# Casts and low parts of the first-half output-projection weights kept behind earlier work of ScalarE and VectorE

## The chip, the cores and the metric

The kernel runs on one core of a Trainium2 chip. The metric is the device time of one execution in microseconds; the time of a kernel is the median of its runs.

## The reference

One inference step of a two-layer model with `D_MODEL` 1024: 128 context tokens and 512 latent tokens, 640 tokens (`T`) in all. In each layer four token mixers stand side by side (grouped-query attention, neighbourhood attention, gated DeltaNet, latent attention "MLA"); the head groups share one input projection and one output projection, and a SwiGLU channel mixer follows. The change touches the output projection alone:

```python
mixed = concat([o_gqa, o_na, o_dn, o_mla], -1)     # 1024 wide, in eight blocks of 128
x = x + gate * (mixed @ w_out)                     # 640 tokens x 1024
```

All matrices are 32-bit floats, and the products are computed to about that precision.

## The kernel before

Matrix products are made of three TensorE passes: each 32-bit operand is split into a rounded part and a low part (what is left), and high x high, high x low, low x high are added. A weight tile is therefore loaded by SyncE into `wst`, rounded by ScalarE into `whi` (line 309), and subtracted by VectorE into `wlo` (line 310). `weights` (line 312) issues these three. `wst` is a ring of three buffers in the pool `wp`; it also holds `xe`, below.

The mixed heads arrive in four pairs `oh` (0 to 3, two blocks of 128 each). The first four blocks are ready well before the last, so the output projection is cut in two. `half_out` (line 2118 on) does the first half while the attention of the latent tokens runs, one tile at a time: for tile `e` of 0 to 5 it loads `wout[l, e, :, 0:4]` (128x512), splits it, loads the residual stream `xe` into a buffer of the ring, makes two half steps of matmuls (256 tokens, then 384 tokens), adds the product to `xe` on VectorE (line 1937) and stores `xe` to scratch memory `dx` (line 2134). The loop over `order` behind the attention does the second halves (called second-half tiles here; six tiles of 128x512, then two whole ones of 128x1024), which read `dx` back into `x`.

TensorE's order is written out by a planner of the kernel: generators for each mixer and for `half_out` take turns by estimated times (`self.od`), and TensorE runs in exactly that order. The instructions of the other engines go to a scheduler, which may move an instruction ahead of others that its engine was given earlier, if its operands allow it. `in_turn` (line 304) marks an instruction that keeps its place in program order. In the kernel before, the split of every weight tile is free to move.

Around the tiles ScalarE runs the exponentials `p` (line 1421), the copies `pt` of transposed exponentials out of the accumulators (line 1456), norms and casts of the neighbourhood attention; VectorE runs row sums and maxima `sm`, reciprocals `sd`, mask additions, low parts and residuals; GpSimd scales (`dg`).

Of the kernel before, what the change touches and what calls it, by code (L numbers as in the profile page):

```python
# [11 lines left out]
F32 = mybir.dt.float32  # L12
# [3 lines left out]
ALU = mybir.AluOpType  # L16
# [272 lines left out]
class _Build:  # L289
# [19 lines left out]
        self.nc.scalar.copy(hi, src)  # L309
        self.nc.vector.tensor_tensor(out=lo, in0=src, in1=hi.bitcast(F32), op=ALU.subtract)  # L310

    def weights(self, src, shape, pool=None, bufs=2, parts=None):

        nc = self.nc
        st = self.wp.tile(shape, F32, tag="wst", name="wst", bufs=3)
        nc.sync.dma_start(out=st, in_=src)
        hi, lo = parts or [(pool or self.wp).tile(shape, F32R, tag=t, name=t, bufs=bufs) for t in ("whi", "wlo")]
        self.split(hi, lo, st)
        n = 1
        for d in shape[1:]:  # L320
            n *= d
        self.od.via(("ACT", 0.1 + n / 1200), ("DVE", 0.07 + n / 960))
        return hi, lo
# [1663 lines left out]
    def mixer(self, l, h, h_st, x, fx, fx_st, P, W, p_side, w_side):  # L1987


        nc, A = self.nc, self.A  # L1990
# [78 lines left out]
        def attention():  # L2069
# [36 lines left out]
            last.extend([od.spawn(self.mla(S, oh, at, ps, 3), 3), _Event()])  # L2106
            e = od.spawn(self.mla_operands(l, mp, mk, xp, ats, ps, S), 1.5)
            od.spawn(half_out(xp, ev_g), 7, True)
            yield e
            mp_st.close()  # L2110
# [5 lines left out]
        wout = lambda q, k: S["oh"][k // 2][:, q, k % 2]  # L2116

        def half_out(xp, ready):

            yield ready  # L2120
            for e in range(KD):
                if all(t.at is not None for t in last):
                    break
                halves.append(e)
                yield "wt", 1
                w = self.weights(A["wout"][l, e, :, 0:4], [128, 4, 128], xp)
                xe = self.wp.tile([128, T], F32, tag="wst", name="xe", bufs=3)
                nc.sync.dma_start(out=xe, in_=xs[:, e])
                for hf in range(2):
                    o = yield from self.half_steps(w, wout, range(4), hf, ps)  # L2130
                    self.residual(l, 2, e, {hf: o}, xe, xe)
                    od.give("fd", at=od.via(("DVE", 0.5)))
                od.give("wt")
                nc.sync.dma_start(out=self.dscr["x1"][:, e], in_=xe)
# [225 lines left out]
```

## Time and profile before

| what | value |
|---|---|
| time, median of 3 runs | 1942.76 us (1941.82 to 1942.79) |
| profiled execution | 1942.35 us, its span 1940.6 us |
| TensorE busy | 1820.8 us (94%) |
| VectorE busy | 1219.8 us (63%) |
| ScalarE busy | 784.7 us (40%) |
| GpSimd busy | 512.7 us (26%) |

The span is the time from the first to the last instruction of the profiled execution; the 1.75 us between it and that execution's time lie around it. Engines run side by side, so a busy time is no part of a sum. A row of a timeline ends with the idle time of its engine just before it and with the instruction that ended that time. The first layer's attention with the six tiles lies at about 320 to 510 us of the span, the second layer's at about 1255 to 1455 us.

### The profile page before, as it was taken

To read this page: it belongs to the slowest core of one execution; us is meant where nothing else is said; L and a number is where in the kernel's file an instruction comes from. 1 tells how busy PE (TensorE), PEld (TensorE's weight loads), DVE (VectorE), ACT (ScalarE), POOL (GpSimd) and SP (SyncE) were. 2 spreads that over 40 slices of the span, in tenths; PEclk is the share of its full clock that TensorE was granted. 3 is DMA by queue.
4 is the path that set the end of the run, shared out by engine and by line. 5 is a ranking of instruction groups with operands and counts; after the bars stand their busy time and mean duration, and the time that the engine had idled before them with its cause. 6 is when DMAs were issued, how large, how long until landed. Compare 5 with 4: busy or idle time off the path is not lost.

```text
span 1940.6 us, 40518 instructions
## 1 busy us (share of the span) xinstructions
PE 1820.8 (94%) x16392; PEld 1714.9 (88%) x16392; DVE 1219.8 (63%) x2488; ACT 784.7 (40%) x1627; POOL 512.7 (26%) x648
## 2 busy tenths in 40 slices
PE   5997998899999999999999999879989999999997
PEld 4986787778899999999998988768779999999997
DVE  6573546676557647747745773566757784774874
ACT  4632123676452212212337432267655541442541
POOL 1221431233220000000021363213324451642731
PEclk9997899999999999999999999989999999999999
DMA  8345323133435525625522232213432222222231
GB/s 302 113 123 135 120 91 98 36 95 88 150 109 176 161 84 181 184 77 192 173 100 92 73 92 66 73 37 78 106 129 89 66 88 76 88 80 82 78 97 55
DMA packets 114171, 210.38 MB, mean 108 GB/s; under 512 B 44160, under 2 KB 61312, under 8 KB 113856
## 3 DMA queue, kind: packets, MB, share of 16 engines
q1 hardware_dynamic: 105920, 202.74, 33.3%
q0 software_dynamic: 2816, 4.72, 1.2%
q8 instruction: 129, 2.11, 0.4%
q10 hardware_dynamic: 5248, 0.33, 0.2%
q14 instruction: 58, 0.48, 0.1%
HBM read 183.14 MB, written 19.89 MB: 105 GB/s over the span
## 4 chain that ended last, share of the span: by engine, by line
PE 77%; DVE 9%; ACT 5%; DMA 5%; issue 2%; SPq 0%; POOL 0%; DVEq 0%; ACTq 0%; POOLq 0%
PE acc L366 55%; PE tacc L366 6%; PE pvo L366 3%; PE ptp L378 3%; PE sc L366 2%; DMA wst<-wout 1%; PE mpart L366 1%; PE invp L366 1%; DVE wlo L310 1%; ACT p L1421 1%; ACT whi L309 1%; DMA wmd<-wmod 1%; DMA wmd<-wmodT 1%; ACT pt L1456 1%; PE ysp L366 1%
## 5 line engine op out<-in xcount | busy, mean ns | idle before, releaser
L366 PE MATMUL acc<-h,whi 128*128 128x256 f32 (+1 forms) x2304 | 453.9, 315 | 3.3 <-ACT h L589 1.4
L366 PEld LDWEIGHTS acc<-h,whi 128*128 128x128 f32 x2304 | 381.1, 191 | 11.9 <-issue 3.4
L309 ACT CAST whi<-wst 128x1024 fp32r<-128x1024 f32 (+3 forms) x164 | 156.9, 958 | 446.1 <-PE acc L366 398.1
L366 PE MATMUL acc<-h,wlo 128*128 128x256 f32 (+1 forms) x1152 | 274.1, 313 | 3.4 <-DVE wlo L310 3.4
L310 DVE TENSOR_TENSOR wlo<-wst,whi 128x1024 fp32r<-128x1024 f32 (+3 forms) x164 | 190.5, 1163 | 99.5 <-ACT whi L309 98.9
L366 PE MATMUL acc<-g,whi 128*128 128x256 f32 (+1 forms) x1128 | 216.7, 309 | 0.3 <-DVE g L310 0.3
L366 PEld LDWEIGHTS acc<-h,wlo 128*128 128x128 f32 x1152 | 211.3, 190 | 5.0 <-DVE wlo L310 3.9
L1937 DVE SCALAR_TENSOR_TENSOR x<-acc,mods,x 128x256 f32<-128x256 f32 (+1 forms) x192 | 75.3, 434 | 196.9 <-PE acc L366 196.8
L556 POOL TENSOR_TENSOR sq<-sq 128x256 f32<-128x256 f32 (+1 forms) x48 | 45.7, 952 | 541.4 <-ACT sq L550 541.1
L366 PEld LDWEIGHTS acc<-g,whi 128*128 128x128 f32 x1128 | 185.9, 188 | 0.5 <-DVE g L310 0.5
L522 DVE SCALAR_TENSOR_TENSOR wmj<-wmd,cb 128x1024 f32<-128x1024 f32 x112 | 136.8, 1222 | 37.2 <-DMA wmd<-wmodT 35.9
L366 PE MATMUL tacc<-whi,h 128*128 128x256 f32 (+1 forms) x640 | 151.0, 317 | 0.3 <-ACT whi L309 0.3
L366 PE MATMUL acc<-h,sw 128*128 128x320 f32 x912 | 143.6, 309 | 0.0
L366 PEld LDWEIGHTS acc<-h,sw 128*128 128x128 f32 x912 | 136.6, 188 | 0.0
L366 PE MATMUL acc<-g,wlo 128*128 128x384 f32 (+1 forms) x564 | 135.2, 309 | 0.0
L366 PEld LDWEIGHTS tacc<-whi,h 128*128 128x128 f32 x640 | 111.2, 194 | 11.1 <-issue 6.4
L366 PE MATMUL acc<-oh,whi 128*128 128x384 f32 (+1 forms) x512 | 115.7, 316 | 5.3 <-ACT whi L309 3.4
L1424 POOL TENSOR_SCALAR dg<-cbase,sd 128x128 f32<-128x128 f32 x96 | 58.7, 612 | 209.3 <-DVE sd L1422 144.7
L366 PE MATMUL acc<-tt,sw 128*128 128x320 f32 x684 | 109.5, 309 | 0.0
L378 PE MATMUL ptp<-cbase,p 128*128 128x128 f32 x512 | 81.6, 286 | 28.2 <-ACT pt L1456 14.4
L366 PEld LDWEIGHTS acc<-g,wlo 128*128 128x128 f32 x564 | 103.3, 188 | 0.0
L366 PEld LDWEIGHTS acc<-tt,sw 128*128 128x128 f32 x684 | 102.6, 188 | 0.0
(361 smaller groups left out, 3426.4 us busy)
## 6 DMA issues: line engine op xcount, KB each, us to landing
wmd<-wmodT SPq DMA_DIRECT2D x56, 512.0 KB
wst<-wg SPq DMA_DIRECT2D x44, 512.0 KB
wst<-wu SPq DMA_DIRECT2D x44, 512.0 KB
wmd<-wmod SPq DMA_DIRECT2D x40, 512.0 KB
wst<-wd SPq DMA_DIRECT2D x34, 448.0 KB
wst<-wfm SPq DMA_DIRECT2D x24, 512.0 KB
wst<-wd SPq DMA_DIRECT2D x16, 512.0 KB
wst<-wtma SPq DMA_DIRECT2D x12, 512.0 KB
```

The costliest lines, as they stand in the source:

```text
L309: self.nc.scalar.copy(hi, src)
L310: self.nc.vector.tensor_tensor(out=lo, in0=src, in1=hi.bitcast(F32), op=ALU.subtract)
L366: self.nc.tensor.matmul(out, lhsT, rhs, start=start, stop=stop)
L378: self.nc.tensor.transpose(out, in_, self.ident)
L522: nc.vector.scalar_tensor_tensor(out=j, in0=st, scalar=1.0, in1=self.cb[:, g], op0=ALU.mult, op1=ALU.mult, accum_out=self.msum[:, e, g:g + 1])
L556: (eng or nc.gpsimd).tensor_tensor(out=self.sq[hf][0], in0=self.sq[hf][0], in1=sq, op=ALU.add)
L1421: nc.scalar.activation(p, s, AF.Exp, bias=m, accum_out=d)
L1424: nc.gpsimd.tensor_scalar(out=dg, in0=self.ident, scalar1=d, scalar2=None, op0=ALU.mult)
L1456: nc.scalar.copy(pt[:, a:a + m].rearrange("p a b -> p (a b)"), tp[:, :128 * m])
L1937: self.nc.vector.scalar_tensor_tensor(out=x_out[:, a:b], in0=o[h][:, a - HB * h:b - HB * h], scalar=m[:, 8 * gate + e, grp:grp + 1], in1=x ...
```

## The change

`weights` takes a flag `late`. With it the cast and the subtraction are issued through `in_turn`, so that ScalarE and VectorE do not run them ahead of what they were given before. Only the call in `half_out` sets it: six tiles in each layer, twelve casts and twelve subtractions. Loads, shapes and arithmetic are the same. Lines from 318 on have a number larger by 4 in the changed kernel.

```diff
--- before.py
+++ after.py
@@ -309,13 +309,17 @@
         self.nc.scalar.copy(hi, src)
         self.nc.vector.tensor_tensor(out=lo, in0=src, in1=hi.bitcast(F32), op=ALU.subtract)
 
-    def weights(self, src, shape, pool=None, bufs=2, parts=None):
+    def weights(self, src, shape, pool=None, bufs=2, parts=None, late=False):
 
         nc = self.nc
         st = self.wp.tile(shape, F32, tag="wst", name="wst", bufs=3)
         nc.sync.dma_start(out=st, in_=src)
         hi, lo = parts or [(pool or self.wp).tile(shape, F32R, tag=t, name=t, bufs=bufs) for t in ("whi", "wlo")]
-        self.split(hi, lo, st)
+        if late:
+            self.in_turn(nc.scalar.copy(hi, st))
+            self.in_turn(nc.vector.tensor_tensor(out=lo, in0=st, in1=hi.bitcast(F32), op=ALU.subtract))
+        else:
+            self.split(hi, lo, st)
         n = 1
         for d in shape[1:]:
             n *= d
@@ -2123,7 +2127,7 @@
                     break
                 halves.append(e)
                 yield "wt", 1
-                w = self.weights(A["wout"][l, e, :, 0:4], [128, 4, 128], xp)
+                w = self.weights(A["wout"][l, e, :, 0:4], [128, 4, 128], xp, late=True)
                 xe = self.wp.tile([128, T], F32, tag="wst", name="xe", bufs=3)
                 nc.sync.dma_start(out=xe, in_=xs[:, e])
                 for hf in range(2):
```

TensorE has the same instructions in the same order in both kernels; the order of the others changes. Names carry a number for each buffer: `whi_5353` is the cast of tile 1 of the first layer, `whi_5588` that of tile 2.

ScalarE, first layer, around tile 1, before:

```order
L1421 ACTIVATE p_5223,sd_5224<-sc_5214,sm_5221 128x768
L309 CAST whi_5588<-wst_5586 128x512
L1421 ACTIVATE p_5248,sd_5249<-sc_5239,sm_5246 128x768
L1484 COPY por_5271<-pvo_5194 128x256
L1456 COPY pt_5321<-ptp_5322 128x512
L362 CAST oh2_3993<-po_5273 128x256
L1456 COPY pt_5332<-ptp_5359 128x512
L1421 ACTIVATE p_5342,sd_5343<-sc_5333,sm_5340 128x768
L1898 ACTIVATE nqp_4933<-nraw_5453 64x128 x2
```

And now:

```order
L1425 ACTIVATE p_5223,sd_5224<-sc_5214,sm_5221 128x768
L1425 ACTIVATE p_5248,sd_5249<-sc_5239,sm_5246 128x768
L1488 COPY por_5271<-pvo_5194 128x256
L1460 COPY pt_5321<-ptp_5322 128x512
L366 CAST oh2_3993<-po_5273 128x256
L1460 COPY pt_5332<-ptp_5359 128x512
L1425 ACTIVATE p_5342,sd_5343<-sc_5333,sm_5340 128x768
L319 CAST whi_5353<-wst_5351 128x512
L1902 ACTIVATE nqp_4933<-nraw_5453 64x128 x2
```

The cast of tile 1 stood some 120 instructions earlier before, and now stands behind the exponential `p_5342`; the cast of tile 2 has left this place for a later one.

ScalarE, second layer, just ahead of the attention (`vn` is the DeltaNet's last norm, `whi_15502` and `whi_15991` are the casts of tiles 0 and 1), before:

```order
L2057 COPY natst_14530<-acc_14407 128x384
L309 CAST whi_15502<-wst_15500 128x512
L1348 COPY ysb_14543<-ysp_14534 128x256
L309 CAST whi_15991<-wst_15989 128x512
L1390 ACTIVATE vn_11407<-dno_13543 128x256 x2
L362 CAST oh1_14630<-og_11402 128x640
```

And now:

```order
L2061 COPY natst_14530<-acc_14407 128x384
L1352 COPY ysb_14543<-ysp_14534 128x256
L1394 ACTIVATE vn_11407<-dno_13543 128x256 x2
L366 CAST oh1_14630<-og_11402 128x640
L309 CAST gk_14830<-gck_14827 128x256
```

Both casts have left the place between the DeltaNet's copies `ysb` and the norm.

SyncE, first layer, end of the attention (`wst_6337`, `wst_6360`, `wst_6401`, `wst_6425` are the first four second-half tiles, `xe_6026` and `xe_6249` tiles 4 and 5), before:

```order
L2128 DMA xe_6249<-xT 128x640
L316 DMA wst_6337<-wout 128x512
L316 DMA wst_6360<-wout 128x512
L316 DMA wst_6401<-wout 128x512
L2134 DMA dx1_79<-xe_6026 128x640
L316 DMA wst_6425<-wout 128x512
L2167 DMA x_6332<-dx1_79 128x640 x5
L2167 DMA x_6332<-xT 128x640 x2
L2134 DMA dx1_79<-xe_6249 128x640
L316 DMA wst_6449<-wout 128x512
L316 DMA wst_6491<-wout 128x512
```

And now:

```order
L2132 DMA xe_6249<-xT 128x640
L2138 DMA dx1_79<-xe_6026 128x640
L316 DMA wst_6337<-wout 128x512
L316 DMA wst_6360<-wout 128x512
L2171 DMA x_6332<-dx1_79 128x640 x3
L316 DMA wst_6401<-wout 128x512
L2171 DMA x_6332<-dx1_79 128x640
L316 DMA wst_6425<-wout 128x512
L2171 DMA x_6332<-dx1_79 128x640
L2138 DMA dx1_79<-xe_6249 128x640
L2171 DMA x_6332<-xT 128x640 x2
L316 DMA wst_6449<-wout 128x512
L316 DMA wst_6491<-wout 128x512
```

The first two loads of second halves move behind the store of tile 4, the third and fourth in between the reads of `x`.

## Rows read from the trace of the kernel before

**Rows 1.** Page: busy us, span share, instructions by engine; then chain shares by line.

```profile
PE 1820.8 (94%) x16392; PEld 1714.9 (88%) x16392; DVE 1219.8 (63%) x2488; ACT 784.7 (40%) x1627; POOL 512.7 (26%) x648
...
PE acc L366 55%; PE tacc L366 6%; PE pvo L366 3%; PE ptp L378 3%; PE sc L366 2%; DMA wst<-wout 1%; PE mpart L366 1%; PE invp L366 1%; DVE wlo L310 1%; ACT p L1421 1%; ACT whi L309 1%; DMA wmd<-wmod 1%; DMA wmd<-wmodT 1%; ACT pt L1456 1%; PE ysp L366 1%
```

**Rows 2.** Chain in order of time, second layer: start us, duration us, what.

```profile
1252.72 4.99 DMA wst<-wout
...
1257.73 0.63 ACT whi L309
...
1258.38 0.69 DVE wlo L310
1259.08 0.34 DVE dno L1389
```

**Rows 3.** Timelines there: start, duration, instruction, [idle before it <-what ended that].

```profile
1255.65 0.86 POOL L1367 TENSOR_TENSOR dno<-dno,ot 128x128 f32<-128x128 f32 x2 [6.44 <-DVE ot L1366]
...
1263.47 0.69 PE L366 MATMUL otp<-cbase,dno 64*64 64x64 f32 x8 [8.24 <-DVE dno L1396]
```

**Rows 4.** Timeline of ScalarE, first layer: first tile's early cast.

```profile
328.22 0.62 ACT L309 CAST whi<-wst 128x512 fp32r<-128x512 f32 x1
```

**Rows 5.** Timeline of TensorE, first layer: before the tiles, and tile 0.

```profile
339.85 0.54 PE L366 MATMUL pvo<-pt,gcv 128*64 128x128 f32 x5 [2.13 <-ACT pt L1456]
...
404.60 0.44 PE L378 MATMUL ptp<-cbase,p 128*128 128x128 f32 x2 [1.51 <-ACT pt L1456]
```

**Rows 6.** Timelines of ScalarE and TensorE, first layer, tile 1.

```profile
435.34 0.91 ACT L1421 ACTIVATE p<-sc,sm 128x768 f32<-128x768 f32 x1
...
434.74 0.29 PE L366 MATMUL acc<-oh,wlo 128*128 128x256 f32 x1
```

**Rows 7.** Timelines of VectorE and TensorE, first layer, tile 2.

```profile
453.06 0.68 DVE L310 TENSOR_TENSOR wlo<-wst,whi 128x512 fp32r<-128x512 f32 x1
...
456.52 0.43 DVE L1911 TENSOR_TENSOR sc<-sc,nat 128x256 f32<-128x256 f32 x1
...
450.91 1.42 PE L366 MATMUL pvo<-pt,mv 128*64 128x128 f32 x21 [0.58 <-ACT pt L1456]
...
454.01 0.28 PE L366 MATMUL acc<-oh,wlo 128*128 128x256 f32 x1
...
455.50 0.66 PE L378 MATMUL ptp<-cbase,p 128*128 128x128 f32 x4 [0.86 <-ACT pt L1456]
456.55 0.44 PE L378 MATMUL ptp<-cbase,p 128*128 128x128 f32 x2 [0.39 <-DVE pt L1454]
```

**Rows 8.** Timelines of VectorE and TensorE, first layer, tile 3.

```profile
470.98 0.69 DVE L1515 TENSOR_REDUCE sm<-psc 128x4 f32<-128x512 f32 x1 [0.69 <-PE psc L366]
...
471.22 0.29 PE L366 MATMUL acc<-oh,wlo 128*128 128x256 f32 x1
```

**Rows 9.** Timeline of TensorE, first layer, just ahead of tile 4.

```profile
483.05 0.66 PE L378 MATMUL ptp<-cbase,p 128*128 128x128 f32 x4 [0.50 <-ACT p L1421]
```

**Rows 10.** First layer's end: chain; window (last: clock, DMA share, GB/s); TensorE.

```profile
505.81 7.06 DMA wst<-wout
...
505.00:510.00 5.00, 5.00 (x38) 5.00 (x38) 1.79 (x4) 0.83 (x2) 0.73 (x1) 1.00 0.91 283
...
513.56 0.51 PE L366 MATMUL acc<-oh,whi 128*128 128x256 f32 x2 [1.14 <-ACT whi L309]
```

**Rows 11.** Window (third from last: clock), second layer; TensorE, second and first layer.

```profile
1362.00:1366.00 4.00, 4.00 (x33) 3.58 (x34) 3.70 (x10) 3.07 (x10) 1.61 (x4) 0.61 0.58 117
...
1361.97 2.83 PE L366 MATMUL pvo<-pt,mv 128*64 128x128 f32 x24 [0.60 <-DVE oh L363]
...
424.78 1.53 PE L366 MATMUL pvo<-pt,mv 128*64 128x128 f32 x24 [0.60 <-DVE oh L363]
```

**Rows 12.** VectorE's line 310 (ns min/median/max), 320 to 510 us; then one timeline row.

```profile
L310 DVE TENSOR_TENSOR wlo<-wst,whi x11: 680/682/693, 328.9 to 504.8; 128x512 fp32r<-128x512 f32 x11
...
1152.86 5.20 DVE L310 TENSOR_TENSOR wlo<-wst,whi 128x1024 fp32r<-128x1024 f32 x1
```

## The prediction

> **What bounds the kernel now.** I read the busy times and the chain first, then the stretches in which the moved instructions stood, engine by engine. TensorE is busy for 94% of the span and holds most of the chain [rows 1]. The change removes no work from it and leaves its instructions in their order. So time can change only where TensorE waits, or where its clock falls. The chain also holds a load of `wst`, casts to `whi` and low parts `wlo`, 1% each: those are the change's own kind of work, and the reader should look for the places where TensorE's idle time ends on them or on something that queued behind them. Twelve casts and twelve low parts are moved (six tiles in each of two layers). They are not dearer later than earlier: all eleven of 128x512 around the first layer's attention took 0.68 to 0.69 us on VectorE [rows 12] and 0.62 us on ScalarE [rows 4]. What counts is which queue each leaves, and whether it is ready where TensorE asks for it.
>
> **What it frees.** (a) Ahead of the first layer's attention ScalarE did the casts of tiles 0 and 1 early, at 328.22 [rows 4] and again six us later, about 80 to 100 us before TensorE used them, between exponentials for which TensorE waits; 2.13 us of such waiting ends on a copy of ScalarE [rows 5]. Both leave: 2 x 0.62 = **-1.2**; bounds 0 (VectorE or a load is next late) and -2.1, the wait itself.
> (b) In the second layer the same two casts stand in front of the DeltaNet's last norm. The cast of tile 1 waits for a load of 4.99 us, then 0.63 us cast and 0.69 us low part, and only then VectorE begins the norm at 1259.08 [rows 2]. Its input was complete when GpSimd ended at 1255.65 + 0.86 = 1256.51, and TensorE waits 8.24 us for what the norm starts [rows 3]. So the norm could begin 1259.08 - 1256.51 = 2.57 us sooner: **-2.5**, since every instruction from the norm to TensorE waits for the one ahead. Bound above: 0, if another operation fills the place.
> (c) At tile 0, TensorE's 1.51 us wait ends on ScalarE's copy `pt` [rows 5]; in the new order that copy stands ahead of an exponential whose place is about 0.8 us, 0.91 with its end [rows 6]: **-0.8** in each layer (0 to -1.5).
> (d) Ahead of tile 4 TensorE waits 0.50 us for an exponential [rows 9] behind the cast and low part of tile 5 and, later, those of the first second-half tiles, which are held too or load later: **-0.5** in each layer (0 to -0.5).
> Freed: 1.2 + 0.8 + 0.5 = 2.5 us in the first layer, 2.5 + 0.8 + 0.5 = 3.8 in the second, 6.3 together.
>
> **What it delays.** (e) Tile 1. Its cast now stands on ScalarE behind the exponential that starts at 435.34 and takes 0.91 [rows 6], hence at 436.28; cast to low part is 1258.38 - 1257.73 = 0.65, and the low part 0.69 [rows 2]; so it is complete at 437.62. TensorE wants it at 434.74 [rows 6]. TensorE works without a pause around that point, and nothing later in its order can pass: **+2.9** in each layer. Queued behind the cast are the next norm on ScalarE and behind the low part a load and a row sum on VectorE, needed some us later. Bounds 0, if TensorE comes that much later in the other layer or shift, and 2.9.
> (f) Tile 2. VectorE's low part is now behind the addition of the neighbourhood mask that starts at 456.52. That addition comes sooner by the 0.58 that TensorE waited [rows 7] behind the cast of tile 3, now gone, and by some of the 0.68 of tile 3's low part. I take the low part as complete at 456.6, so TensorE's instruction of 454.01 is 2.6 late; but its next waits, 0.86 and 0.39, are swallowed [rows 7]: 2.6 - 1.25 = **+1.35** in each layer. Bounds 0 and 1.95 (no gain from tile 3's low part).
> (g) Tile 3. Its low part follows the row sum that starts at 470.98 and takes 0.69 [rows 8], so it lasts from about 471.6 to 472.3; TensorE wants it at 471.22 [rows 8]: **+1.1** in each layer, bounds 0 and 1.1.
> (h) The end of the attention. The ring of three buffers now holds each weight tile until its late cast, so SyncE cannot place the loads of the second halves early. Before, three of them started ahead of the fifth store; now two come behind it, and the third and fourth stand among the reads of `x`. There the DMA engines already moved 283 GB/s at a share of 0.91, and a load of 7.06 us ended the wait of 1.14 for the fifth second-half tile [rows 10]. Two loads of 0.26 MB more in that stretch are 0.52 MB / 283 GB/s = 1.85 us; that the first two casts now stand ahead of the last copies of ScalarE adds a little: **+2.0** in each layer, bounds 1.0 (half falls into free DMA time) and 3.0.
> Delayed: 2.9 + 1.35 + 1.1 + 2.0 = 7.35 in each layer.
>
> **The clock.** Tile-sized waits can cost more than their length. In the second layer TensorE's clock fell after a wait that ended in 0.60 at 1361.97: 24 matmuls took 2.83 us where the same 24 took 1.53 behind the same 0.60 in the first, and a stretch of 4 us ran at 0.61, which is the lower level, 1.2 GHz, for most of it [rows 11]. So the price is 2.83 - 1.53 = 1.30 to 0.39 x 4.00 = 1.56, say 1.5, and the same wait cost it in one layer and not in the other. The new waits that are long enough are three: tile 1 in each layer and the end of the first. I count one fall: **+1.5**, bounds 0 and 4.5.
>
> **Sum.** First layer 7.35 - 2.5 = 4.85, second 7.35 - 3.8 = 3.55, clock 1.5: +9.9 us. The profiled execution took 1942.35 us (span 1940.6 and 1.75 around it), 0.4 below the median of the runs: 1942.35 + 9.9 = **1952.3**.
>
> **Rivals.** *Faster.* ScalarE and VectorE, freed, run far enough ahead, or TensorE comes late enough, that (e) to (h) cost nothing; only the 6.3 us stay: 1936.1. It decides at tile 1: TensorE would have to reach it 2.9 us later against ScalarE than now. For it: TensorE does wait for ScalarE before and after these places [rows 5, 7]. Against: at tile 1 the cast's new place hangs on an exponential of the same step, so a general shift moves both.
> *No change.* Tile 1 stalls, but (f) to (h) vanish in other waits, and the clock holds: 5.8 - 6.3 = -0.5, 1941.9. For it: tiles 2 and 3 are close to waits already there. Against: the loads at the end are bound by bandwidth.
> *More clock.* All three long waits bring the clock down and the end costs its upper bound: 3.0 more of clock and 2 x 1.0 more at the ends, 1957.3. One layer of two showed such a fall.
> *The port.* One low part of 128x1024 took 5.20 us while GpSimd worked, though two of half that size are 2 x 0.68 = 1.36 [rows 12]. Were the moved low parts that TensorE waits for (tiles 1 and 3, both layers) hit alike, each would take (5.20 - 1.36) / 2 = 1.9 more: 7.7, 1960.0. Against it: none of the eleven took over 693 ns [rows 12], with GpSimd at work in that stretch. The Trainium skill, page "SBUF — State Buffer", section "SBUF: two separate sides", has the rule for it: VectorE with two inputs in SBUF and GpSimd hold one pair of ports exclusively, and the loser stands still for the other's whole instruction. By that rule the moved low parts could be hit and the sum would be 17.6 instead of 9.9; the trace shows it at one size and not at the other.
> *The hold does nothing* is excluded: the order of the built kernel has the casts elsewhere.
>
> **How the numbers follow.** Forecast 0.54, more clock 0.12, port 0.06, no change 0.14, faster 0.14. A measurement of this kernel tells 0.2%, 3.9 us, from no change; so slower is 0.54 + 0.12 + 0.06 = 0.72, same 0.14, faster 0.14. The range leaves out the faster case and a few in a hundred above: 1940 (the no-change case in it) to 1960 (the port's).
>
> **What would show it.** Right: TensorE idle some 2.2 to 2.9 us before tile 1's matmuls, put down to `whi` or `wlo`, in both layers; its wait of 8.24 down to about 5.7; a longer wait than 1.14 at the fifth second-half tile. Wrong: no wait at tile 1 (then the faster case), or a wait of 8.24 that stays, because something else fills the place in front of the norm; or a wait for `oh` rather than for a load at the end.

## The result: slower by 0.8%, within the range

| | before | after |
|---|---|---|
| median | 1942.29 us (1938.83 to 1942.79, 4 runs) | 1954.57 us (1952.13 to 1955.86, 4 runs) |
| profiled execution | 1942.35 us, span 1940.6 | 1955.86 us, span 1954.1 |

The ratio is 1.008, with a 95% interval of 1.005 to 1.0109: 12.3 us more. The forecast was 1952.3, 9.9 us more than the profiled execution of before, in a range of 1940 to 1960. A second comparison on another chip (below) gave 1.009.

The page of after has the same work on every engine (busy times in us, instructions; then the clock in 40 slices):

```profile
PE 1831.7 (94%) x16392; PEld 1723.2 (88%) x16392; DVE 1216.3 (62%) x2488; ACT 784.9 (40%) x1627; POOL 517.4 (26%) x648
...
PEclk8997998999999999999999999999899999999999
```

TensorE is busy 10.9 us longer than before [rows 1] with the same 16392 matmuls. That is already a sign that not only waits were added: the same matmuls took longer, and the mean granted clock of TensorE was 0.971 here, 0.976 in the profile of before.

**Tile 1.** ScalarE's and TensorE's timelines of after, first layer (start, duration, instruction, idle time before it):

```profile
430.96 0.90 ACT L1425 ACTIVATE p<-sc,sm 128x768 f32<-128x768 f32 x1
...
431.86 0.61 ACT L319 CAST whi<-wst 128x512 fp32r<-128x512 f32 x1
...
429.69 0.60 PE L382 MATMUL ptp<-cbase,p 128*128 128x128 f32 x4
432.51 0.50 PE L370 MATMUL acc<-oh,whi 128*128 128x256 f32 x2 [2.22 <-ACT whi L319]
433.28 0.39 PE L370 MATMUL acc<-oh,wlo 128*128 128x256 f32 x1 [0.27 <-DVE wlo L320]
...
435.38 0.63 PE L382 MATMUL ptp<-cbase,p 128*128 128x128 f32 x2
...
437.39 0.52 PE L370 MATMUL acc<-oh,whi 128*128 128x384 f32 x2
```

The cast stands behind the exponential, as the order said, and TensorE, done with the four transposes of 429.69, waits 2.22 us for the cast and 0.27 for the low part. How much later everything is comes from setting the same matmul of both traces side by side. Before, TensorE had:

```profile
434.06 0.60 PE L378 MATMUL ptp<-cbase,p 128*128 128x128 f32 x4
...
437.21 0.51 PE L366 MATMUL acc<-oh,whi 128*128 128x384 f32 x2
```

The transposes stand at 434.06 before and at 429.69 here, 4.37 us ahead (the start of this execution went faster); the tile's second half step stands at 437.21 before and at 437.39 here, 0.18 behind. So 4.55 us were lost between them. The waits are 2.49 of that. Most of the rest, 1.7 us by the working in the table below, is the clock. Two windows of after show it (window, us, busy us and instructions of PE, PEld, DVE, ACT, POOL, then granted clock, DMA share, GB/s):

```profile
427.00:433.00 6.00, 3.78 (x38) 3.04 (x32) 3.42 (x9) 4.76 (x11) 1.82 (x3) 1.00 0.65 220
433.00:437.00 4.00, 3.73 (x16) 3.52 (x16) 1.08 (x3) 0.59 (x2) 0.00 (x0) 0.57 0.54 174
```

Up to the tile it is 1.00, the upper level; behind the wait it is 0.57, most of four microseconds at 1.2 GHz.

**Tiles 2 and 3.** TensorE's timeline, first layer:

```profile
455.81 0.50 PE L370 MATMUL acc<-oh,whi 128*128 128x256 f32 x2 [1.98 <-ACT whi L319]
457.30 0.48 PE L370 MATMUL acc<-oh,wlo 128*128 128x256 f32 x1 [0.99 <-DVE wlo L320]
...
475.56 0.39 PE L370 MATMUL acc<-oh,wlo 128*128 128x256 f32 x1 [0.94 <-DVE wlo L320]
```

Before, none of these three had a wait; tile 2's two waits of 0.86 and 0.39 behind it [rows 7] are gone, as the prediction had it.

**Second layer.** TensorE's timeline:

```profile
1267.11 0.69 PE L370 MATMUL otp<-cbase,dno 64*64 64x64 f32 x8 [5.62 <-DVE dno L1400]
...
1375.92 0.80 PE L370 MATMUL acc<-oh,whi 128*128 128x256 f32 x2 [2.22 <-ACT whi L319]
...
1400.23 0.50 PE L370 MATMUL acc<-oh,whi 128*128 128x256 f32 x2 [1.97 <-ACT whi L319]
1401.72 0.39 PE L370 MATMUL acc<-oh,wlo 128*128 128x256 f32 x1 [0.99 <-DVE wlo L320]
...
1419.93 0.55 PE L370 MATMUL acc<-oh,wlo 128*128 128x256 f32 x1 [0.95 <-DVE wlo L320]
...
1464.68 0.80 PE L370 MATMUL acc<-oh,whi 128*128 128x256 f32 x2 [2.72 <-ACT whi L309]
```

The first row answers to [rows 3]: 8.24 us have become 5.62, 2.62 us less. The next four repeat the first layer's waits to 0.01 us; only the 0.27 for tile 1's low part has no counterpart. The last is the fifth second-half tile, where the wait was long before the change, too:

```profile
1453.41 0.50 PE L366 MATMUL acc<-oh,whi 128*128 128x256 f32 x2 [2.27 <-ACT whi L309]
```

**The end of the first layer.** SyncE's issues and the fifth second-half tile on TensorE:

```profile
499.20 0.33 SPq L2138 DMA_DIRECT2D dx<-xe  x1
501.36 0.81 SPq L316 DMA_DIRECT2D wst<-wout  x2
504.71 1.78 SPq L2171 DMA_DIRECT2D x<-dx  x3
506.59 0.38 SPq L316 DMA_DIRECT2D wst<-wout  x1
...
507.54 0.38 SPq L316 DMA_DIRECT2D wst<-wout  x1
...
514.03 1.68 SPq L316 DMA_DIRECT2D wst<-wout  x2
...
518.59 0.50 PE L370 MATMUL acc<-oh,whi 128*128 128x256 f32 x2 [1.69 <-ACT whi L309]
```

Before, SyncE had issued the first three of these loads from 482.44 on:

```profile
482.44 9.07 SPq L316 DMA_DIRECT2D wst<-wout  x3
```

Now the first two are issued at 501.36, behind the store of tile 4, the third and fourth at 506.59 and 507.54 between the reads of `x`, and the wait at the fifth second-half tile is 1.69 us instead of 1.14 [rows 10].

### The profile page after: what moved, and what is told of

Same layout as the page of the kernel before. It is cut to its first block, busy times and chain, and to the rows that moved or that the text cites. A ratio compares the mean times of both kernels' runs of the same rounds, so it can differ in the third digit from the quotient of the medians.

```text
span 1954.1 us, 40517 instructions
## 1 busy us (share of the span) xinstructions
PE 1831.7 (94%) x16392; PEld 1723.2 (88%) x16392; DVE 1216.3 (62%) x2488; ACT 784.9 (40%) x1627; POOL 517.4 (26%) x648
## 4 chain that ended last, share of the span: by engine, by line
PE 80%; DVE 7%; ACT 5%; DMA 4%; issue 2%; SPq 1%; POOL 1%; ACTq 0%; DVEq 0%; POOLq 0%
PE acc L370 56%; PE tacc L370 7%; PE sc L370 3%; PE ptp L382 3%; PE pvo L370 3%; PE mpart L370 1%; PE invp L370 1%; DMA wst<-wout 1%; ACT p L1425 1%; DVE wlo L310 1%; ACT whi L309 1%; PE ysp L370 1%; ACT pt L1460 1%; PE spp L370 1%; PE opp L370 1%
## 5 line engine op out<-in xcount | busy, mean ns | idle before, releaser
L309 ACT CAST whi<-wst 128x1024 fp32r<-128x1024 f32 (+3 forms) x152 | 149.7, 985 | 443.9 <-PE acc L370 393.0
L310 DVE TENSOR_TENSOR wlo<-wst,whi 128x1024 fp32r<-128x1024 f32 (+3 forms) x152 | 179.1, 1178 | 96.7 <-ACT whi L309 95.8
L370 PE MATMUL acc<-oh,whi 128*128 128x384 f32 (+1 forms) x512 | 121.2, 327 | 14.9 <-ACT whi L319 8.4
L370 PEld LDWEIGHTS acc<-oh,whi 128*128 128x128 f32 x512 | 89.1, 201 | 19.1 <-ACT whi L319 9.8
```

Of the source, the lines that this page charges most:

```text
L370: self.nc.tensor.matmul(out, lhsT, rhs, start=start, stop=stop)
```

## Where the time went

For each stretch the table gives the sum of the shifts between the same matmuls of the profile before and of two profiles of the changed kernel (the second is from the second chip), without the clock; and the clock by itself, worked out as half of TensorE's busy time while the granted clock was at its lower level, after minus before. Stretches are named by the steps of the prediction.

| step | forecast | after, first profile | second profile | clock, first | clock, second |
|---|---|---|---|---|---|
| (a) ahead of the first layer's attention | -1.2 | -0.6 | -0.9 | -0.7 | -0.1 |
| (b) in front of the norm, second layer | -2.5 | -2.6 | -2.6 | 0 | 0 |
| (c) tile 0, first layer | -0.8 | +0.4 | +0.4 | 0 | 0 |
| (c) tile 0, second layer | -0.8 | +0.4 | +0.4 | 0 | 0 |
| (d) ahead of tile 4, first, second layer | -0.5, -0.5 | -0.5, -1.0 | -0.5, -1.0 | 0 | 0 |
| (e) tile 1, first layer | +2.9 | +2.9 | +2.9 | +1.7 | +1.7 |
| (e) tile 1, second layer | +2.9 | +1.9 | +2.3 | +3.3 | +1.6 |
| (f) tile 2, first, second layer | +1.35, +1.35 | +1.6, +1.3 | +1.6, +1.4 | +1.7, +1.7 | +1.7, +1.5 |
| (g) tile 3, first, second layer | +1.1, +1.1 | +0.5, +0.3 | +0.3, +0.4 | 0, +1.7 | +3.1, 0 |
| (h) end, first, second layer | +2.0, +2.0 | +3.9, +0.9 | +2.9, +0.7 | 0, +1.7 | +1.7, 0 |
| both attentions in all (320 to 600 and 1250 to 1520 us before) | +8.4 and clock +1.5 | +6.4 | +5.7 | +12.9 | +13.8 |

The last row holds also what lies between the steps. For the clock that is 1.8 and 2.6 us: in both profiles it fell just ahead of tile 1 in the first layer (+1.7), behind waits of 1.57 and 1.55 and then 0.60 us that are as long before, where it held; in both the fall of before at 1362 [rows 11] is missing (-1.6); and 1.7 and 2.4 us lie elsewhere in the second layer.

The attentions lose 19.3 and 19.5 us in these two profiles against the one of before. Outside them, where the change moved no cast, single executions differ from one another by some us (here -5.7 and +0.8); in the medians one sees 12.3 us on the first chip and 17.1 (1956.24 to 1939.18) on the second. So the waits came to 2.0 and 2.7 us less than forecast, and the clock to eight or nine times the forecast.

## The experiments

Each ran beside the kernel before on the same chip; ratios are to that.

### Which tiles: t01_late, t25_late

```diff
-                w = self.weights(A["wout"][l, e, :, 0:4], [128, 4, 128], xp, late=True)
+                w = self.weights(A["wout"][l, e, :, 0:4], [128, 4, 128], xp, late=e < 2)
```

> Only tiles 0 and 1 are held back; tiles 2 to 5 are free as before. Theory A (waits of TensorE at the tiles, each with a fall of its clock): the two places ahead of the attention are freed (-1.2 and -2.6 us), tile 1 waits 2.5 us in each layer, and the clock falls behind each wait (3.4 to 6.8 us at the lower level, 1.7 to 3.3 us each): -3.8 + 5.0 + 5.0 = +6, about 1948. Theory B (the late loads at the end of the attention cost the time): the loads stand as before, so only the freed places show, about 1938. Theory C (run-to-run differences of the clock, not the waits): as before plus or minus 3.

1944.11 us (12 runs), ratio 1.0024 (1.0006 to 1.0043). TensorE's timeline has the wait of tile 1, to 0.01 us, and tile 2's first matmul without one:

```profile
432.12 0.50 PE L370 MATMUL acc<-oh,whi 128*128 128x256 f32 x2 [2.22 <-ACT whi L319]
...
453.56 0.40 PE L370 MATMUL acc<-oh,whi 128*128 128x256 f32 x2
```

In its profile the steps at tile 1 are +4.56 and +5.05 us, as in after (+4.56 and +5.11), nothing follows at tiles 2 and 3 or at the end of the first layer, and the place in front of the norm gives the same -2.62. The second layer's end is 2.6 us shorter than in the profile of before, where one load of `wst` took 9.12 us against 7.91 here; since that differs from run to run, I count it to neither side. Theory B, by which the late loads at the end would hold the whole loss, expected some 4 us less than the kernel before (1938); the run took more than it, with the whole interval above 1, so B is out. Theory A had the sign and the places; its +6 us is 4.7 by the ratio.

```diff
-                w = self.weights(A["wout"][l, e, :, 0:4], [128, 4, 128], xp, late=True)
+                w = self.weights(A["wout"][l, e, :, 0:4], [128, 4, 128], xp, late=e >= 2)
```

> Only tiles 2 to 5 are held back; the casts of tiles 0 and 1 stand early as before. Theory A: no wait at tile 1, waits of 2 to 3 us at tile 2 and of 0.9 us at tile 3 in each layer, net of waits that vanish +1.7 and +0.7 and with about one fall of the clock per layer, 1.7 us each, and about 1 us at each layer's end: +8, about 1950. Theory B: nearly the whole of the difference, about 1955 with nothing freed at the start. Theory C: about 1942.

1948.93 us (10 runs), ratio 1.0048 (1.003 to 1.0066). No wait at tile 1; 1.97 and 0.98 us at tile 2 and 0.95 at tile 3 of the first layer, and the second layer's attention loses 4.5 us. The two halves together, 0.24% and 0.48%, make 0.72%, beside 0.8% and 0.9% of the whole.

### Which engine: after_again, cast_only, low_only

> The changed kernel once more, beside the next three on one chip. Ratio to the kernel before 1.005 to 1.011; if the first comparison owed much to chance, nearer to 1.0.

1956.24 us (6 runs), ratio 1.009 (1.0072 to 1.0108).

```diff
-            self.in_turn(nc.vector.tensor_tensor(out=lo, in0=st, in1=hi.bitcast(F32), op=ALU.subtract))
+            nc.vector.tensor_tensor(out=lo, in0=st, in1=hi.bitcast(F32), op=ALU.subtract)
```

> Only the casts on ScalarE are held; the low parts on VectorE are free again. A low part needs its cast, so it cannot come much earlier. If the hold on ScalarE is the cause: as the changed kernel, ratio 1.006 to 1.010, with the same waits of 2.2 and 2 us at tiles 1 and 2. If the hold on VectorE is: near 1.0.

1959.33 us (5 runs), ratio 1.011 (1.0092 to 1.0127), a little above the range expected; its interval overlaps that of the changed kernel. TensorE's waits for a cast in the first layer, at tiles 1 and 2:

```profile
439.38 0.51 PE L370 MATMUL acc<-oh,whi 128*128 128x256 f32 x2 [2.22 <-ACT whi L319]
462.51 0.50 PE L370 MATMUL acc<-oh,whi 128*128 128x256 f32 x2 [2.00 <-ACT whi L319]
```

```diff
-            self.in_turn(nc.scalar.copy(hi, st))
+            nc.scalar.copy(hi, st)
```

> Only the low parts on VectorE are held; the casts on ScalarE are free and stand as before. If the hold on ScalarE is the cause: no wait for a cast at tile 1, small waits for low parts (under 1 us) at tiles 2 and 3, one fall of the clock at most, and the late loads at the end, since a weight buffer is held until its low part: ratio 1.0 to 1.004. If the hold on VectorE is: as the changed kernel.

1944.82 us (12 runs), ratio 1.0037 (1.0022 to 1.0052). Tile 1's first matmul has no wait; the norm's wait went from 8.24 to 6.17 us, 2.07 of the 2.62 that it lost in after, so it was mostly the low part, not the cast, that kept the norm back:

```profile
431.93 0.48 PE L370 MATMUL acc<-oh,whi 128*128 128x256 f32 x2
...
1265.65 0.69 PE L370 MATMUL otp<-cbase,dno 64*64 64x64 f32 x8 [6.17 <-DVE dno L1400]
```

The hold on ScalarE makes the waits for casts and the larger part of the loss: a low part cannot come before its cast, so holding the cast holds both. It is not the whole: holding the low parts alone costs 0.37%, clear of 1. The smaller waits for low parts that I expected at tiles 2 and 3 did not show: TensorE's waits there end on exponentials (1.66 and 1.33 us). Nor did "one fall of the clock at most" hold: in its profile the clock fell five times between 399 and 425 and between 1345 and 1419, behind other waits of 1.5 to 1.8 us, and only once there in the profile of before [rows 11].

### The clock: fill_wait, fill123

```diff
+        for _ in range(fill):
+            self.nc.tensor.matmul(o, rhs(0, ks[0])[:, 0:128], rhs(0, ks[0])[:, SPLIT[h]], start=True, stop=True)
...
+                    o = yield from self.half_steps(w, wout, range(4), hf, ps, fill=20 if e == 1 and hf == 0 else 0)
```

> As the changed kernel, with 20 matmuls of 256 columns, whose result is thrown away, just ahead of tile 1's first matmul in both layers: TensorE works through the 2.2 us in which it waited. Theory A: the wait itself stays as delay, but the clock does not fall behind it, which gives back 1.7 us in the first layer and up to 3.3 in the second: about 1950. If the falls of the clock do not hang on that wait: as the changed kernel, 1954.6, or a little more.

1950.67 us (6 runs), ratio 1.0064 (1.0041 to 1.0087): about 0.2% less than the changed kernel's 1.009, but the intervals overlap, and 1.0064 is also what 1954.6, the other outcome, would be beside the first 1942.3. So the time alone does not decide. In its profile the clock holds at tile 1 in both layers and falls at tiles 2 and 3, where nothing was put. So the next run fills those too (20, 24 and 8 matmuls at tiles 1, 2, 3):

```diff
+                    o = yield from self.half_steps(w, wout, range(4), hf, ps, fill=(0, 20, 24, 8, 0, 0)[e] if hf == 0 else 0)
```

> As the run with discarded matmuls ahead of tile 1, now also ahead of tile 2 (24 of them, about 2.9 us) and tile 3 (8, about 1 us), in both layers. The delays stay, TensorE is busy through them. If the falls of the clock hang on these waits: none of the falls behind tiles 1 to 3, so some 3 us less than with tile 1 alone, ratio 1.003 to 1.006. If they come from elsewhere: as with tile 1 alone, 1.0064, or above.

1946.54 us (12 runs), ratio 1.0046 (1.0028 to 1.0064). TensorE's timeline at tile 1; line 704 is the matmuls whose result is thrown away, in the place of the 2.22 us:

```profile
432.38 2.63 PE L704 MATMUL acc<-oh 128*128 128x256 f32 x20
434.85 0.50 PE L370 MATMUL acc<-oh,whi 128*128 128x256 f32 x2
435.62 0.39 PE L370 MATMUL acc<-oh,wlo 128*128 128x256 f32 x1 [0.27 <-DVE wlo L320]
```

And windows around tiles 1, 2 and 3 of both layers, the third number from the end being the granted clock:

```profile
433.00:440.00 7.00, 6.73 (x62) 6.11 (x63) 2.85 (x6) 3.40 (x9) 0.60 (x1) 1.00 0.66 225
456.00:463.00 7.00, 6.59 (x69) 6.08 (x68) 4.89 (x16) 2.96 (x8) 3.94 (x6) 1.00 0.38 99
473.00:480.00 7.00, 7.00 (x67) 6.37 (x67) 4.55 (x11) 4.22 (x15) 1.75 (x3) 1.00 0.17 47
...
1374.00:1381.00 7.00, 6.74 (x51) 6.27 (x50) 3.38 (x8) 3.81 (x10) 0.60 (x1) 1.00 0.79 251
1397.00:1404.00 7.00, 6.58 (x62) 6.25 (x62) 5.94 (x16) 3.49 (x8) 4.38 (x7) 1.00 0.46 122
1414.00:1421.00 7.00, 6.56 (x60) 5.88 (x60) 4.72 (x12) 4.71 (x17) 1.98 (x3) 1.00 0.31 84
```

It is 1.00 in all six. The changed kernel has more idle time and less work and takes 1.009; this one has the same delays, more work, and takes 1.0046. So about half of the loss is the clock behind these waits. The profile agrees: its two attentions lose 8.6 us against before, where the changed kernel's lose 19.3 and 19.5, and the clock by itself, worked out as in the table, comes to -0.6 us instead of 12.9 and 13.8.

How often it falls shows over all profiles in which these waits stand: behind those of tiles 1 and 2, 2.2 to 3 us with short work inside, 18 times of 18 (tile 1 in four profiles and tile 2 in five, two layers each), for 1.5 to 1.7 us, or about 3.2 where it lasted on; behind tile 3's 0.94 us, 6 times of 10. The length of a wait alone does not decide it: at the end of the first layer's attention in `fill123` TensorE waits 2.63 us for a residual, and the window around it (second row) is at 1.00. No run here shows why.

```profile
508.99 0.47 PE L370 MATMUL acc<-oh,whi 128*128 128x256 f32 x2 [2.63 <-DVE xe L1943]
...
507.00:514.00 7.00, 5.01 (x36) 5.04 (x37) 3.44 (x8) 2.28 (x5) 0.14 (x1) 1.00 0.98 354
```

### Freed without the stall: pipe6, pipe2, pipe2_again

Both issue the next tile's load, cast and low part between the two half steps of a tile, held as in the change, with TensorE's order the same. `pipe6` does so for tiles 1 to 5; `pipe2` for tile 1 alone (2 in the place of 6), tiles 2 to 5 being free to move. The lines that issue them early (the lines that then use them are left out):

```diff
...
                     od.give("fd", at=od.via(("DVE", 0.5)))
+                    if hf == 0 and e + 1 < 6:
+                        got[e + 1] = self.weights(A["wout"][l, e + 1, :, 0:4], [128, 4, 128], xp, late=True, plan=False)
...
```

> All tiles held, each issued one half step of the tile before earlier (tiles 1 to 5 between the two half steps of the tile ahead). Cast and low part are then complete when TensorE comes: no waits at tiles 1 to 3, and the places ahead of the attention stay freed (-1.2 and -2.6 us). Against pipe2, which left tiles 2 to 5 free: the loads at the end of each layer's attention may be up to 1 us later. Ratio 0.994 to 0.999. If holding costs in itself, apart from the waits at the tiles, above 1.0.

1933.86 us (12 runs), ratio 0.9969 (0.9956 to 0.9982).

> Tile 0 is held back as in the changed kernel; tile 1's cast and low part are issued between the two half steps of tile 0, held behind what came before, so they are complete long before tile 1; tiles 2 to 5 are free. Theory A: the freed places stay (-1.2 and -2.6 us), no wait at tile 1, no further fall of the clock: about 1938. If a freed place brings nothing because something else is next late: about 1942.

1929.52 us (6 runs), ratio 0.9953 (0.9936 to 0.997).

> The kernel that holds tiles 0 and 1 alone and issues tile 1 half a tile early, once more. If its gain is no chance of one chip: ratio 0.993 to 0.997 again. If it was: nearer to 1.0.

1931.66 us (12 runs), ratio 0.9961 (0.9945 to 0.9977). So both are faster than the kernel before, too. ScalarE's cast of tile 1 and TensorE's rows at it, then the norm's wait:

```profile
414.91 0.66 ACT L319 CAST whi<-wst 128x512 fp32r<-128x512 f32 x1
...
432.55 0.60 PE L383 MATMUL ptp<-cbase,p 128*128 128x128 f32 x4
432.90 0.48 PE L371 MATMUL acc<-oh,whi 128*128 128x256 f32 x2
...
1258.30 0.69 PE L371 MATMUL otp<-cbase,dno 64*64 64x64 f32 x8 [5.62 <-DVE dno L1401]
```

The cast is done 17 us before the tile, the matmul follows its transposes at once, and the 2.62 us in front of the norm stay gained. It gains more than the 3.8 us of (a) and (b): in `pipe2`'s two profiles another 2.1 and 2.5 us go in the thirty microseconds behind the norm, and 1.6 where the clock fell at 1362 before [rows 11] and does not here. What these two hang on was not tested; the changed kernel, with the same 5.62 in front of the norm, does not have the first (+0.1 and +0.3 us there).

## Why the prediction was right, point by point

- (b): the mechanism and the size. 2.62 us came in every profile in which casts and low parts leave the norm's front, and 2.07 with the casts left there.
- (a): within its bounds, 0.6 to 0.9 without the clock, but not as told. The wait of 2.13 [rows 5] is gone, and a few us on, where TensorE had no wait before, one of about the same length ends on another copy `pt`; what is gained lies in shorter waits around it. TensorE in after:

```profile
338.50 1.66 PE L382 MATMUL ptp<-cbase,p 128*128 128x128 f32 x6 [2.59 <-ACT pt L1460]
```

- (c) was wrong. The wait of 1.51 [rows 5] did shrink by 0.8, to 0.73, but four us further on TensorE now waits 0.73 for another copy of ScalarE, and the stretch as a whole lost 0.4 us:

```profile
398.13 0.44 PE L382 MATMUL ptp<-cbase,p 128*128 128x128 f32 x2 [0.73 <-ACT pt L1460]
...
402.62 0.44 PE L382 MATMUL ptp<-cbase,p 128*128 128x128 f32 x2 [0.73 <-ACT mkp L1801]
```

- (d): -0.5 and, in the second layer, -1.0; the first layer's number is luck. The wait named there, 0.50 [rows 9], still stands, in both profiles of the changed kernel, at 0.47; the 0.5 us is the sum of a wait of 0.21 just behind it and smaller shifts. In the second layer the wait did shrink, from 0.50 to 0.12. TensorE in after, first layer:

```profile
486.71 0.66 PE L382 MATMUL ptp<-cbase,p 128*128 128x128 f32 x4 [0.47 <-ACT p L1425]
```

- (e): the waits are 2.49 us, forecast 2.9 with what follows: right in the first layer. In the second, 1.9 to 2.3: a wait of 0.30 a few us behind tile 1 is gone there.
- (f): right in size, 1.3 to 1.6, and the two waits behind it were swallowed as forecast. But of the 2.97 us that TensorE waits, 1.98 are for the cast on ScalarE; the forecast had only VectorE's low part late.
- (g): half, 0.3 to 0.5, since TensorE's next wait was swallowed, which I had left out.
- (h): outside its bounds of 1.0 and 3.0 in both layers of the first profile: 2.9 to 3.9 in the first layer and 0.7 to 0.9 in the second. In the first, 0.65 and 0.69 us came at the fifth second-half tile, the place of the forecast. About 1 us in both profiles came some 40 us later, at a wait for `h`, which `pipe2_again` has too with tiles 2 to 5 free, so it is not shown to be the late loads'. In the second layer the fifth tile's wait had been long before (2.27); in kernels with tiles 2 to 5 free it was 0.97 to 1.75, so what the late loads cost there cannot be told from this spread.
- The clock is the term that was mis-sized: one fall of three, 1.5 us, against 12.9 and 13.8. The price of a fall was near (1.5 to 1.7 measured, 3.2 where it lasted on); the number was not. I took "one layer of two" from one wait of 1.54 + 0.60 us, where the clock fell 10 times of 16 over all profiles, and applied it to the waits at the tiles, which brought it down 18 times of 18 at tiles 1 and 2, and did not count tiles 2 and 3 as places.
- The rule on the shared ports ("SBUF — State Buffer", "SBUF: two separate sides" in the Trainium skill) made no difference here by the trace of after: tile 1's held low part took its usual time (0.73 us; all twelve held low parts took 0.67 to 0.73, beside 0.68 to 0.69 [rows 12]), so the 7.7 us of that rival did not come.

That the total came so near is in large part luck. The waits were 2 to 3 us below the forecast and the clock 11 to 12 above; that leaves 19.3 and 19.5 us in the attentions where 9.9 were forecast, and the first comparison came nearer only with the rest of the program, which ran 5.7 us faster in its profile. The second chip's 17.1 us, put on 1942.35, would be 1959.4, just inside the range. What the runs showed is nearer to the rival "More clock" (1957.3) than to the forecast: it had every long wait bring the clock down, though at three places alone.

## What to carry to other kernels

An operand's preparation that stands early in an engine's queue costs the queue's next users, and one that stands at its use costs the consumer: look for the place between, here half a tile ahead, which was worth more than either end. When a change makes the bounding engine wait, price each wait as its length and a possible fall of the clock of its own, count the places one by one, and look in the profile whether it fell there. Holding one engine's instruction holds every engine downstream of it, and the buffers it reads, and so the loads that want them.

## What was not expected of the hardware

The granted clock fell behind every one of the 18 waits of 2.2 to 3 us at tiles 1 and 2 and behind 6 of 10 waits of 0.94 us at tile 3, in a kernel whose TensorE is busy 94% of the span. Matmuls put into these gaps, their results thrown away, kept it at 1.00 there, so that the kernel that does more work was the faster one.
